# Score matmuls of two differential heads in one run of 24, and one pool of six PSUM banks for products and scores

## The chip, the cores and the metric

One NeuronCore of a Trainium2 chip runs the whole program. The metric is the device time of one execution in microseconds; it is given as the median of several runs. The engines are named as the profile names them: PE is the matmul engine (PEld its weight loads), DVE the vector engine, ACT the scalar engine, POOL and SP the two that only set constants and issue transfers here.

## The reference, cut to what matters

Two layers of an encoder over 256 tokens of width 2048. Each layer has a differential attention of 8 heads, a latent attention (MLA) of 8 heads, a gate for each, an output product, a SwiGLU feed-forward and a gated per-layer embedding.

```python
h = rmsnorm(x, g_mix[i])
z = h @ w_in[i]
dq, dk, dv, cq, ckv, kr, ga, gb = jnp.split(z, split_at, axis=-1)
# differential attention: 8 heads, each with two halves (c) of width 64
scores = jnp.einsum('bqhcd,bkhcd->bhcqk', qb, kh).astype(jnp.float32) * scale
probs = jax.nn.softmax(scores, axis=-1)
weights = probs[:, :, 0] - lam * probs[:, :, 1]
return jnp.einsum('bhqk,bkhe->bqhe', weights.astype(v.dtype), v)
```

So each differential head needs two score maps (one for each half of 64 features), two softmaxes, and their weighted difference.

## The kernel before

Activations lie with features on the 128 partitions and the 256 tokens on the free axis, each as two fp32r parts side by side: a high part and the rest (`ua`, `ub`, `fa`, `fb` hold 2 x 256 columns). Weights come from HBM as pieces of 128 x 1024 (`piece`, lines 182 to 208): ACT makes the high part `whi` (line 201), DVE the rest `wlo` (line 78, the helper that records every DVE addition and subtraction). Both have a ring of three buffers, so the split of a piece waits until PE has finished the piece three before it. A product (`product`, line 234) multiplies 16 chunks of a weight tile with 16 chunks of activations into one PSUM bank: for each chunk a matmul of 512 columns with `whi` (line 226) and one of 256 columns with `wlo` (line 230). `joined` (line 254) then takes the product out of its bank: ACT copies one half (`join`, line 256), DVE adds the other half (`a`), and with that addition the bank is free. `pair` (line 246) makes two small products from one piece.

PSUM has eight banks. Before the change four of them are for products (pool `ps_mm`, tile `mm`), two for scores (`ps_s`, tile `S`) and two for transposes and outputs of heads (`ps_at`, tile `at`). A pool gives a tile one of its free banks when the program is built, and the first matmul into it waits for the last reader of what was there.

The differential stage comes once in each layer. `beside()` (line 617) is a list of fillers, cut into steps by its yields: two steps for each of the heads 2 to 7 (first `keys_up`, two small products for the latent keys, or `narrow` for the shared rope key, or nothing; then `queries_keys`, a query product and a key product with their rotation), and four steps with a gate and two small products each. `settle` (line 709) normalizes four heads' outputs. `pipelined` (line 718) weighs head h+1 between two steps and puts out head h after it. `diff_weights` (line 684) does one head: `scores` (line 420) runs its 12 score matmuls, `exps` (line 431) its two softmaxes (a DVE reduction for the row maxima, two ACT exponentials for each map), and then ACT scales and DVE combines the two maps. The score matmuls have 64 rows only; `scores` lets those of the two halves alternate, so that they lie on the upper and the lower half of the array and run side by side. `turned` (line 440) transposes the weights, and `diff_out` (line 695) multiplies them with the values.

The order within an engine is made by the build's scheduler from the order of the code, except where `tc.keep_in_program_order` fixes it. Each engine then works strictly in that order, with semaphores between the engines.

Of the kernel before, what the change touches and what calls it, by code (L numbers as in the profile page):

```python
# [15 lines left out]
AF = mybir.ActivationFunctionType  # L16
ALU = mybir.AluOpType
AX = mybir.AxisListType

P = 128  # L20
T = 256
# [3 lines left out]
DH = 8  # L25
# [31 lines left out]
def encoder(ctx, tc, x, p, positions, cols, lams, wq, wk, wv, wcq, wckv, wkr, wga, wgb,  # L57
            w_q_up, w_kn, w_v, w_bd, w_bm, w_out, w_gate, w_up, w_down, w_pin, w_pg, rope_c, out):
    nc = tc.nc
    V, A, PE = nc.vector, nc.scalar, nc.tensor  # L60
    PSUM = bass.MemoryType.PSUM
    pool = lambda name, bufs=1, **k: ctx.enter_context(tc.tile_pool(name=name, bufs=bufs, **k))
# [1 line left out]
    wts = pool("wts")  # L64
    tmp = pool("tmp")
    stat = pool("stat")
    ps_mm = pool("ps_mm", 4, space=PSUM)
    ps_s = pool("ps_s", 2, space=PSUM)
    ps_at = pool("ps_at", 2, space=PSUM)

    def scratch(tag, bufs, n=T):
# [2 lines left out]
    def bank(ps=ps_at, tag="at", name="at", shape=(P, 2 * T)):  # L74
        return ps.tile(list(shape), F32, tag=tag, name=name)
# [4 lines left out]
    def stt(o, a, s, b, op0, op1):  # L80
        return V.scalar_tensor_tensor(out=o, in0=a, scalar=s, in1=b, op0=op0, op1=op1)

    def ts(o, a, s1, s2, op0, op1=ALU.bypass):
        return V.tensor_scalar(out=o, in0=a, scalar1=s1, scalar2=s2, op0=op0, op1=op1)  # L84
# [16 lines left out]
    def operand(t):  # L101
        return t.rearrange("p c t -> p (c t)")
# [24 lines left out]
    halves = rc[:, 4 : 4 + P]  # L127
# [28 lines left out]
    neg_lam = const.tile([P, DEPTH], F32, name="neg_lam")  # L156
    gsub = const.tile([P, DEPTH], F32, name="gsub")
    lam_s = const.tile([P, DEPTH, 2], F32, name="lam_s")
    lam_in = tmp.tile([P, 2, T], F32, tag="E", name="lam_in", bufs=2).rearrange("p l (f d) -> p l f d", f=4)

# [212 lines left out]
    krs = [const.tile([P, gap + 2 * T], F32R, name=f"kr{j}")[:, gap:] for j, gap in enumerate((KR_GAP, 0))]  # L373
# [43 lines left out]
    def three(q, k):  # L417
        return [(q[:, :T], k[:, T:]), (q[:, T:], k[:, :T]), (q[:, :T], k[:, :T])]

    def scores(*maps):  # L420


        Ss = [bank(ps_s, "S", "S", (P, 2, T)) for _ in maps]
        for b in range(2):
            for j in range(len(maps[0])):
                for S, pairs in reversed(list(zip(Ss, maps))):
                    q, k = pairs[j]
                    PE.matmul(S[:, b, :], q[:, b * P : (b + 1) * P], k, start=j == 0, stop=j == len(pairs) - 1)  # L428
        return Ss

    def exps(S, E, scale):

        nm, sm, rs = (stat.tile([P, 2], F32, tag=t, name=t, bufs=4) for t in ("nm", "sm", "rsum"))
        V.tensor_reduce(out=nm, in_=S, axis=AX.X, op=ALU.max, negate=True)
        ts(nm, nm, scale, None, ALU.mult)
        for b in range(2):
            last_exp[0] = A.activation(E[:, b, :], S[:, b, :], AF.Exp, bias=nm[:, b : b + 1], scale=scale, accum_out=sm[:, b : b + 1])  # L437
        V.reciprocal(out=rs, in_=sm)
        return rs
# [17 lines left out]
    def head(vals, kb, h):  # L457
        return vals[:, kb, h // 4, (h % 4) * P : (h % 4 + 1) * P]

    def weights(tag="E", dt=F32):  # L460
        return tmp.tile([P, 2, T], dt, tag=tag, name=tag, bufs=2)
# [65 lines left out]
    for L in range(DEPTH):  # L527
# [43 lines left out]
        qk = [(ub[h], operand(fa(h, F32R))) for h in range(DH)]  # L571
# [13 lines left out]
        qn, kn, qr = [], [], ub[14:]  # L585
# [94 lines left out]
        fill = beside()  # L680
        od, ods = [], ub[:8]
        ssd = stat.tile([P, 2 * DH], F32, tag="ssd", name="ssd", bufs=1)

        def diff_weights(h):
            q, k = qk[h]
            E = [weights(), weights("E1")]
            halves = [slice(c * 64, (c + 1) * 64) for c in range(2)]
            r = [exps(S, e, 0.125) for S, e in zip(scores(*(three(q[d], k[d]) for d in halves)), E)]
            ts(r[1], r[1], neg_lam[:, L : L + 1], None, ALU.mult)
            for b in range(2):  # L690
                A.activation(E[0][:, b, :], E[0][:, b, :], AF.Copy, scale=r[0][:, b : b + 1])
                stt(E[0][:, b, :], E[1][:, b, :], r[1][:, b : b + 1], E[0][:, b, :], ALU.mult, ALU.add)
            return E[0]

        def diff_out(h, W):
            wt = turned(W)
            yield
            o = bank()
            for b in range(2):
                for kb in range(2):  # L700
                    PE.matmul(o[:, b * P : (b + 1) * P], wt[:, kb, b * P : (b + 1) * P], head(vd, kb, h), start=kb == 0, stop=kb == 1)  # L701
            f = fa(h)
            od.append(f[:, 0, :])
            A.activation(od[h], o[:, :T], AF.Copy)
            for b in range(2):
                A.activation(f[:, 1, :P], od[h][:, b * P : (b + 1) * P], AF.Square, accum_out=ssd[:, 2 * h + b : 2 * h + b + 1])
# [12 lines left out]
        def pipelined(weigh, put, heads, step):  # L719
            W = weigh(0)  # L720
            for h in range(heads):
                step()
                nxt = weigh(h + 1) if h + 1 < heads else None
                out = put(h, W)
                next(out)
                step()
                next(out, None)
                W = nxt

        pipelined(diff_weights, diff_out, DH, lambda: next(fill, None))  # L730
        for _ in fill:
            pass
        vm, = (v for v in values(w_v[L], ckv) if v is not None)
# [3 lines left out]
        def mla_weights(h):  # L737
            E = weights()
            t = slice(h % 2 * T, (h % 2 + 1) * T)
            S, = scores(three(qn[h], kn[h]) + [(qr[h // 2][:, t], krs[1][:, t]), (qr[h // 2][:, t], krs[0][:, :T])])  # L740
            r = exps(S, E, MLA_SCALE)
            for b in range(2):
                ts(E[:, b, :], E[:, b, :], r[:, b : b + 1], None, ALU.mult)
            return E
# [48 lines left out]
        for part, (f0, f1) in enumerate(FF_PARTS):  # L793
            for f in range(f0, f1):
# [50 lines left out]
    parts, banks, tiles_ = {}, {}, {}  # L845
# [14 lines left out]
    for n in ends:  # L860
        m = banks[n, 1] = bank(ps_mm, "mm", "mm")
# [40 lines left out]
    def transposed(b, q, into, c0=0, c1=4):  # L902
        for c in range(c0, c1):
            tc.keep_in_program_order(PE.transpose(into[:, c * P : (c + 1) * P], xT[:, 4 * q + c, b * P : (b + 1) * P], ident))  # L904
        return into
# [17 lines left out]
            scaled(o[:, k * 2 * T : (k + 1) * 2 * T], src, col, engine)  # L923
        tc.keep_in_program_order(nc.sync.dma_start(out[b, :, q * 2 * T : (q + len(srcs)) * 2 * T], o))

    def S_bank():
        return operand(bank(ps_s, "S", "S", (P, 2, T)))

    def mm_bank():
        return bank(ps_mm, "mm", "mm")  # L930

    def steps(which, n):
        for _ in range(n):
            tc.keep_in_program_order(next(which))
# [6 lines left out]
    column = factors(0)  # L941
    for which, n in ((column, 2), (third, 1), (column, 2), (second, 1), (column, 1), (second, 1), (column, 1), (third, 1), (column, 1), (third, 1), (column, 1)):
        steps(which, n)
    t0 = [transposed(0, q, get()) for q, get in enumerate((S_bank, S_bank, mm_bank, mm_bank))]
    t1 = [transposed(1, q, mm_bank()) for q in range(2)]
    steps(factors(1), 8)
    t1.append(transposed(1, 2, bank()))
# [1 line left out]
    with tc.issue_after(gains[-1].ins):  # L949
        for q, m in ((1, 1), (2, 2)):  # L950
            store(0, q, t0[q : q + m], cols_[0], (A, A))
    t1.append(transposed(1, 3, S_bank()))
    for q in (0, 2):
        store(1, q, t1[q : q + 2], cols_[1], (V, A))

# [87 lines left out]
```

## Time and profile before

| | |
|---|---|
| median of 3 runs | 2826.22 us (2826.18 to 2826.6) |
| the profiled execution, its own time | 2825.67 us |
| its span | 2823.8 us |
| PE busy | 2815.6 us (100% of the span) |
| DVE busy | 2078.3 us (74%) |
| ACT busy | 1532.2 us (54%) |
| runs of 12 score matmuls of 64 rows | 16 (8 in a layer), 192 matmuls |
| differential stage, layer 0 / layer 1 | first score run at 106.12 us / at 1509.42 us |

PE is busy from 1 us to the end, so the time is the sum of what PE's instructions take from one to the next. What is not PE matters only where it makes PE wait. A view of groups gives the mean duration of an instruction. Instructions of DVE and ACT overlap a little with the next, so the distance from one start to the next, which the timeline shows, is shorter than that duration.

### The profile page before, as it was taken

The numbers are of one execution on the slowest core, as the hardware profiler recorded it, in microseconds if no ns is written. First come the engines' busy times: TensorE is split into PE (matmuls) and PEld (weight loads), VectorE is DVE, ScalarE is ACT, GpSimd is POOL, SyncE is SP. The second block draws the span as 40 slices with busy tenths as digits, with TensorE's granted clock in tenths as the row PEclk, the third lists the DMA queues.
The fourth block names the chain that finished last, engine by engine and source line by source line (L and its number), as shares of the span: only waits on it lengthen the run. The fifth ranks groups of instructions, "written<-read, shape, count | busy, mean of one in ns | idle before, by whom it ended". The sixth has DMA issues, their size and how long they took to land.

```text
span 2823.8 us, 43997 instructions
## 1 busy us (share of the span) xinstructions
PE 2815.6 (100%) x16691; PEld 2488.8 (88%) x16691; DVE 2078.3 (74%) x3574; ACT 1532.2 (54%) x2556; POOL 2.0 (0%) x16
## 2 busy tenths in 40 slices
PE   9999999999999999999999999999999999999998
PEld 8888988888888888888888889888888888888888
DVE  8898668776666666677869976687766666666777
ACT  7676556554444444455646765465544444444556
POOL 0000000000000000000000000000000000000000
PEclk9999999999999999999999999999999999999999
DMA  7544455555665565565664454555556655655654
GB/s 247 176 160 172 158 186 197 194 194 194 187 200 194 187 195 199 193 192 193 194 194 165 157 173 159 194 197 193 193 194 189 200 193 185 202 195 193 192 193 154
DMA packets 158325, 531.37 MB, mean 188 GB/s; under 512 B 17184, under 2 KB 25376, under 8 KB 158112
## 3 DMA queue, kind: packets, MB, share of 16 engines
q1 hardware_dynamic: 157680, 527.96, 56.9%
q8 instruction: 131, 2.15, 0.3%
q14 instruction: 82, 0.67, 0.1%
q10 hardware_dynamic: 432, 0.59, 0.1%
HBM read 526.39 MB, written 2.10 MB: 187 GB/s over the span
## 4 chain that ended last, share of the span: by engine, by line
PE 100%; DVE 0%; DVEq 0%; issue 0%
PE mm L226 61%; PE mm L230 31%; PE S L428 1%; PE mmv L502 1%; PE mmv L503 1%; PE mmv L501 1%; PE at L446 1%; PE at L701 1%; PE mm L848 0%; PE at L757 0%; PE mm L414 0%; PE at L517 0%; PE at L716 0%; PE mmv L472 0%; PE at L339 0%; PE mm L904 0%
## 5 line engine op out<-in xcount | busy, mean ns | idle before, releaser
L201 ACT ACTIVATE whi<-w 128x1024 fp32r<-128x1024 f32 (+2 forms) x1038 | 1064.2, 1026 | 1226.7 <-issue 593.3
L78 DVE TENSOR_TENSOR wlo<-w,whi 128x1024 fp32r<-128x1024 f32 (+2 forms) x1038 | 1224.7, 1180 | 647.9 <-ACT whi L201 640.5
L226 PE MATMUL mm<-ub,whi 128*128 128x512 f32 x3936 | 1340.5, 389 | 0.0
L226 PE MATMUL mm<-ua,whi 128*128 128x512 f32 x3712 | 1274.0, 390 | 0.0
L230 PE MATMUL mm<-ub,wlo 128*128 128x256 f32 x3936 | 1084.6, 276 | 0.0
L230 PE MATMUL mm<-ua,wlo 128*128 128x256 f32 x3712 | 1027.6, 277 | 0.0
L226 PEld LDWEIGHTS mm<-ub,whi 128*128 128x128 f32 x3936 | 737.8, 188 | 152.7
L226 PEld LDWEIGHTS mm<-ua,whi 128*128 128x128 f32 x3712 | 696.3, 188 | 141.5
L230 PEld LDWEIGHTS mm<-ub,wlo 128*128 128x128 f32 x3936 | 738.9, 188 | 1.3
L230 PEld LDWEIGHTS mm<-ua,wlo 128*128 128x128 f32 x3712 | 697.0, 188 | 2.0
L78 DVE TENSOR_TENSOR a<-mm,join 128x256 f32<-128x256 f32 (+1 forms) x423 | 174.2, 415 | 1.7 <-ACT join L877 1.4
L256 ACT ACTIVATE join<-mm 128x256 f32<-128x256 f32 x452 | 165.2, 367 | 6.4 <-PE mm L230 5.7
L78 DVE TENSOR_TENSOR xT<-xT,mm 128x256 f32<-128x256 f32 x256 | 106.7, 419 | 41.5 <-PE mm L230 37.7
L78 DVE TENSOR_TENSOR a<-a,row 128x256 f32<-128x256 f32 (+1 forms) x209 | 87.4, 422 | 5.9
L78 DVE TENSOR_TENSOR a<-a 128x256 f32<-128x256 f32 x120 | 50.8, 425 | 4.0
L78 DVE TENSOR_TENSOR ua<-a,ua 128x256 fp32r<-128x256 f32 x120 | 49.8, 417 | 1.0 <-ACT ua L264 1.0
L264 ACT ACTIVATE ua<-a 128x256 fp32r<-128x256 f32 x120 | 48.2, 403 | 2.6 <-DVE a L78 2.6
L437 ACT ACTIVATE E<-S,nm 128x256 f32<-128x256 f32 x96 | 44.1, 471 | 8.2 <-DVE nm L84 8.2
L501 PE MATMUL mmv<-whi,ua 128*128 128x512 f32 x124 | 47.0, 391 | 0.0
L502 PE MATMUL mmv<-whi,ua 128*128 128x512 f32 x124 | 47.0, 392 | 0.0
L503 PE MATMUL mmv<-wlo,ua 128*128 128x512 f32 x124 | 41.2, 391 | 0.0
L78 DVE TENSOR_TENSOR ssq<-ssq,sq 128x256 f32<-128x256 f32 x96 | 40.0, 417 | 0.3 <-ACT sq L294 0.3
(213 smaller groups left out, 1211.8 us busy)
## 6 DMA issues: line engine op xcount, KB each, us to landing
w<-in_w_gate SPq DMA_DIRECT2D x176, 512.0 KB, 4.6
w<-in_w_up SPq DMA_DIRECT2D x176, 512.0 KB, 4.6
w<-in_w_down SPq DMA_DIRECT2D x128, 512.0 KB, 4.3
w<-in_wga SPq DMA_DIRECT2D x64, 512.0 KB, 3.8
w<-in_wgb SPq DMA_DIRECT2D x64, 512.0 KB, 3.7
w<-in_w_out SPq DMA_DIRECT2D x64, 512.0 KB, 4.5
w<-in_w_pg SPq DMA_DIRECT2D x64, 512.0 KB, 4.7
w<-in_w_down SPq DMA_DIRECT2D x64, 384.0 KB, 3.6
```

The costliest lines, as they stand in the source:

```text
L78: return V.tensor_tensor(out=o, in0=a, in1=b, op=op)
L201: last_split[:] = A.activation(hi[:, s], w[:, s], AF.Copy), tt(lo[:, s], w[:, s], hi[:, s].bitcast(F32), ALU.subtract)
L226: lead = PE.matmul(acc, hi[:, s], u, start=start, stop=False)
L230: rest = PE.matmul(acc[:, T:], lo[:, s], u[:, :T], start=False, stop=stop)
L256: A.activation(t, acc[:, T:], AF.Copy)
L264: return A.activation(hi, src, AF.Copy), tt(lo, src, hi.bitcast(F32), ALU.subtract)
L428: PE.matmul(S[:, b, :], q[:, b * P : (b + 1) * P], k, start=j == 0, stop=j == len(pairs) - 1)
L437: last_exp[0] = A.activation(E[:, b, :], S[:, b, :], AF.Exp, bias=nm[:, b : b + 1], scale=scale, accum_out=sm[:, b : b + 1])
L446: PE.transpose(tp[:, kb, b * P : (b + 1) * P], W[:, b, kb * P : (kb + 1) * P], ident)
L501: PE.matmul(banks[k][b], xh, hi[:, s], start=c == 0, stop=False)
L502: PE.matmul(banks[k][b], xl, hi[:, s], start=False, stop=False)
L503: last_mm[:] = [PE.matmul(banks[k][b], xh, lo[:, s], start=False, stop=c == n - 1)]
```

## The change

1. `ps_s` is gone, and `ps_mm` has six banks in place of four. A score map takes a bank of the same pool as a product.
2. `scores` takes several heads and runs them one after the other, kept in program order where there is more than one. `diff_weights(h0)` takes the heads h0+1 and h0: 24 score matmuls in four banks, and then both heads' softmaxes.
3. A written loop over pairs of heads replaces `pipelined` in the differential stage: two steps at first; then for each pair the scores, two steps (one for the last pair), the transposes of both heads, one step, both heads' outputs, and one step (none for the last pair). So a pair's scores stand one or two steps after the keys of its second head.
4. The transposes at the end of the kernel take banks of the pool of six where they took score banks.

The MLA stage calls `scores` with one head and one map, as before.

```diff
-    ps_mm = pool("ps_mm", 4, space=PSUM)
-    ps_s = pool("ps_s", 2, space=PSUM)
+    ps_mm = pool("ps_mm", 6, space=PSUM)
...
-    def scores(*maps):
-        Ss = [bank(ps_s, "S", "S", (P, 2, T)) for _ in maps]
-        for b in range(2):
-            for j in range(len(maps[0])):
-                for S, pairs in reversed(list(zip(Ss, maps))):
-                    q, k = pairs[j]
-                    PE.matmul(S[:, b, :], q[:, b * P : (b + 1) * P], k, start=j == 0, stop=j == len(pairs) - 1)
+    def scores(*heads):
+        Ss = [[S_bank() for _ in maps] for maps in heads]
+        for banks, maps in zip(Ss, heads):
+            for b in range(2):
+                for j in range(len(maps[0])):
+                    for S, pairs in reversed(list(zip(banks, maps))):
+                        q, k = pairs[j]
+                        m = PE.matmul(S[:, b, :], q[:, b * P : (b + 1) * P], k, start=j == 0, stop=j == len(pairs) - 1)
+                        if len(heads) > 1:
+                            tc.keep_in_program_order(m)
         return Ss
...
-        def diff_weights(h):
-            q, k = qk[h]
-            E = [weights(), weights("E1")]
+        def diff_weights(h0):
             halves = [slice(c * 64, (c + 1) * 64) for c in range(2)]
-            r = [exps(S, e, 0.125) for S, e in zip(scores(*(three(q[d], k[d]) for d in halves)), E)]
+            pairs = [[three(qk[h][0][d], qk[h][1][d]) for d in halves] for h in (h0 + 1, h0)]
+            Ws = []
+            for Ss in scores(*pairs):
+                E = [weights(), weights("E1")]
+                r = [exps(S, e, 0.125) for S, e in zip(Ss, E)]
...
+                Ws.append(E[0])
+            return Ws[::-1]
...
-        pipelined(diff_weights, diff_out, DH, lambda: next(fill, None))
+        steps_on(2)
+        for h in range(0, DH, 2):
+            last = h + 2 == DH
+            Ws = diff_weights(h)
+            steps_on(1 if last else 2)
+            outs = [diff_out(h + j, Ws[j]) for j in range(2)]
+            for part in outs:
+                next(part)
+            steps_on(1)
+            for part in outs:
+                next(part, None)
+            if not last:
+                steps_on(1)
```

How the instructions stand after the change, at three places of layer 0 (layer 1 has the same). Lines of the changed kernel are shifted: its 77 is line 78 of before, 225 and 229 are 226 and 230, 437 is 428, 445 is 434, 588 is 577, 730 is 716.

**PE, around the first score run.** Before, the run of head 0 stands within the small products for the latent keys (`ub` 104 and 105 are the latent, `ua` the normalized input):

```order
L226 MATMUL mm<-ub_104,whi 128x512
L230 MATMUL mm<-ub_104,wlo 128x256
L428 MATMUL S<-fa_640,ub_92 128x256 x12
L226 MATMUL mm<-ub_105,whi 128x512
L230 MATMUL mm<-ub_105,wlo 128x256
L226 MATMUL mm<-ub_104,whi 128x512
```

Now the run of 24 (first head 1, then head 0) stands behind the key product of head 2. Behind it come the two small products `mm_1473` and `mm_1485` of the next step, 8 matmuls, and then the query product of head 3, `mm_1497`:

```order
L225 MATMUL mm_1473<-ub12_101,whi_1469 128x512 [waits PE_49]
L229 MATMUL mm_1473<-ub12_101,wlo_1468 128x256
L225 MATMUL mm_1473<-ub13_102,whi_1469 128x512
L229 MATMUL mm_1473<-ub13_102,wlo_1468 128x256
L225 MATMUL mm_1485<-ub12_101,whi_1469 128x512 [waits DVE_49]
L229 MATMUL mm_1485<-ub12_101,wlo_1468 128x256
L225 MATMUL mm_1485<-ub13_102,whi_1469 128x512
L229 MATMUL mm_1485<-ub13_102,wlo_1468 128x256
L225 MATMUL mm_1497<-ua0_73,whi_1500 128x512 [waits DVE_49]
```

The run has moved 72 matmuls later and is twice as long. Its four score maps hold four of the six banks, `mm_1473` and `mm_1485` get the other two, and `mm_1497` is given the bank of `mm_1473`. The wait on DVE in the last row is for the addition that takes `mm_1473` out of that bank.

**DVE, at the same place.** Before, the two reductions of head 0 stand between additions, and the addition that frees the bank of the small product (`mm_1297`) comes a few rows behind them, long before that bank is wanted again:

```order
L434 TENSOR_REDUCE nm_1270<-S_1256 128x2
L434 TENSOR_REDUCE nm_1278<-S_1257 128x2
L78 TENSOR_TENSOR ub9_101<-fb5_648,ub9_101 128x256
L78 TENSOR_TENSOR ub10_102<-fb6_649,ub10_102 128x256
L78 TENSOR_TENSOR ub11_103<-fb6_649,ub11_103 128x256
L78 TENSOR_TENSOR ub1_93<-a_1171,ub1_93 128x256
L577 STREAM_SHUFFLE sh_1246<-a_1244 128x256
L78 TENSOR_TENSOR a_1305<-mm_1297,join_1303 128x256
```

Now the addition out of `mm_1473` is the last of these rows. `wlo_1521` is the second half of head 3's query weights, `mm_1337` the key product of head 2 that PE ends just before the run, `mm_1393` to `mm_1396` are the score maps:

```order
L77 TENSOR_TENSOR wlo_1521<-w32_1520,whi_1522 128x1024
L77 TENSOR_TENSOR a_1384<-mm_1337,join_1382 128x256
L77 TENSOR_TENSOR a_1328<-a_1328,sh_1330 128x256
L445 TENSOR_REDUCE nm_1423<-mm_1393 128x2
L445 TENSOR_REDUCE nm_1431<-mm_1394 128x2
L588 STREAM_SHUFFLE sh_1386<-a_1384 128x256
L445 TENSOR_REDUCE nm_1446<-mm_1395 128x2
L77 TENSOR_TENSOR ub2_91<-a_1328,ub2_91 128x256
L445 TENSOR_REDUCE nm_1454<-mm_1396 128x2
L83 TENSOR_SCALAR nm_1423<-nm_1423 128x2
L83 TENSOR_SCALAR nm_1431<-nm_1431 128x2
L77 TENSOR_TENSOR a_1481<-mm_1473,join_1479 128x256
```

Four reductions, a weight split and six smaller instructions now stand ahead of the addition that frees the bank. At the second pair (heads 2 and 3) DVE has the same picture: `mm_1729` is the key product ahead of the run, and PE's query product `mm_1889`, behind the two small products `mm_1865` and `mm_1877`, waits for the last row:

```order
L77 TENSOR_TENSOR wlo_1913<-w32_1912,whi_1914 128x1024
L77 TENSOR_TENSOR a_1776<-mm_1729,join_1774 128x256
L445 TENSOR_REDUCE nm_1815<-mm_1785 128x2
L445 TENSOR_REDUCE nm_1823<-mm_1786 128x2
L445 TENSOR_REDUCE nm_1838<-mm_1787 128x2
L588 STREAM_SHUFFLE sh_1778<-a_1776 128x256
L445 TENSOR_REDUCE nm_1846<-mm_1788 128x2
L83 TENSOR_SCALAR nm_1815<-nm_1815 128x2
L77 TENSOR_TENSOR a_1873<-mm_1865,join_1871 128x256
```

Behind the third run stands the product of `narrow` (16 matmuls of 512 columns), which takes one bank, and the next product's bank is freed by an addition that stands ahead of the four reductions.

**PE, at the last pair.** The run of heads 6 and 7 is cut in two by a pair of transposes of 128 rows that belong to `settle`:

```order
L229 MATMUL mm<-ub_100,wlo 128x256
L437 MATMUL mm<-fa_644,ub_96 128x256 x7
L730 MATMUL at<-ident,fa_2029 128x128 x2
L437 MATMUL mm<-fa_644,ub_96 128x256 x5
L437 MATMUL mm<-fa_643,ub_95 128x256 x12
L225 MATMUL mm<-ua_73,whi 128x512
```

So a layer has five stretches of 64-row matmuls where it had eight, and the cut falls between the two matmuls of a side-by-side pair.

More of the change, by code (lines that the diff above doesn't have):

```diff
@@ L418, in three, with mm_bank, S_bank @@
         return [(q[:, :T], k[:, T:]), (q[:, T:], k[:, :T]), (q[:, :T], k[:, :T])]
-    def scores(*maps):
-        Ss = [bank(ps_s, "S", "S", (P, 2, T)) for _ in maps]
-        for b in range(2):
-            for j in range(len(maps[0])):
-                for S, pairs in reversed(list(zip(Ss, maps))):
-                    q, k = pairs[j]
-                    PE.matmul(S[:, b, :], q[:, b * P : (b + 1) * P], k, start=j == 0, stop=j == len(pairs) - 1)
+    def mm_bank():
+        return bank(ps_mm, "mm", "mm")
+    def S_bank():
+        return mm_bank().rearrange("p (b t) -> p b t", b=2)
+    def three(q, k):
+        return [(q[:, :T], k[:, T:]), (q[:, T:], k[:, :T]), (q[:, :T], k[:, :T])]
+    def scores(*heads):
[8 more added lines that the diff above has]
+                            tc.keep_in_program_order(m)
         return Ss
@@ L682, in encoder @@
         ssd = stat.tile([P, 2 * DH], F32, tag="ssd", name="ssd", bufs=1)
-        def diff_weights(h):
-            q, k = qk[h]
-            E = [weights(), weights("E1")]
+        def diff_weights(h0):
             halves = [slice(c * 64, (c + 1) * 64) for c in range(2)]
-            r = [exps(S, e, 0.125) for S, e in zip(scores(*(three(q[d], k[d]) for d in halves)), E)]
[L689 to L693, printed above, removed]
+            pairs = [[three(qk[h][0][d], qk[h][1][d]) for d in halves] for h in (h0 + 1, h0)]
[3 more added lines that the diff above has]
+                r = [exps(S, e, 0.125) for S, e in zip(Ss, E)]
+                ts(r[1], r[1], neg_lam[:, L : L + 1], None, ALU.mult)
+                for b in range(2):
+                    A.activation(E[0][:, b, :], E[0][:, b, :], AF.Copy, scale=r[0][:, b : b + 1])
+                    stt(E[0][:, b, :], E[1][:, b, :], r[1][:, b : b + 1], E[0][:, b, :], ALU.mult, ALU.add)
+                Ws.append(E[0])
+            return Ws[::-1]
         def diff_out(h, W):
@@ L728, in pipelined, with steps_on @@
                 W = nxt
-        pipelined(diff_weights, diff_out, DH, lambda: next(fill, None))
+        def steps_on(n):
+            for _ in range(n):
+                next(fill)
+        steps_on(2)
[11 more added lines that the diff above has]
+                steps_on(1)
         for _ in fill:
@@ L739, in mla_weights @@
             t = slice(h % 2 * T, (h % 2 + 1) * T)
-            S, = scores(three(qn[h], kn[h]) + [(qr[h // 2][:, t], krs[1][:, t]), (qr[h // 2][:, t], krs[0][:, :T])])
+            (S,), = scores([three(qn[h], kn[h]) + [(qr[h // 2][:, t], krs[1][:, t]), (qr[h // 2][:, t], krs[0][:, :T])]])
             r = exps(S, E, MLA_SCALE)
@@ L924, in store @@
         tc.keep_in_program_order(nc.sync.dma_start(out[b, :, q * 2 * T : (q + len(srcs)) * 2 * T], o))
[L926 to L930, printed above, removed]
     def steps(which, n):
@@ L943, in encoder @@
         steps(which, n)
-    t0 = [transposed(0, q, get()) for q, get in enumerate((S_bank, S_bank, mm_bank, mm_bank))]
+    t0 = [transposed(0, q, get()) for q, get in enumerate((mm_bank,) * 4)]
     t1 = [transposed(1, q, mm_bank()) for q in range(2)]
@@ L951, in encoder @@
             store(0, q, t0[q : q + m], cols_[0], (A, A))
-    t1.append(transposed(1, 3, S_bank()))
+    t1.append(transposed(1, 3, mm_bank()))
     for q in (0, 2):
```

## Prediction

> **What bounds the kernel now.** I read the page first, then PE's waits, then the chain that ended last, and at last the timeline of the differential stage.
>
> ```profile
> PE 2815.6 (100%) x16691; PEld 2488.8 (88%) x16691; DVE 2078.3 (74%) x3574; ACT 1532.2 (54%) x2556; POOL 2.0 (0%) x16
> PEclk9999999999999999999999999999999999999999
> ```
>
> ```profile
> engine line waited for: us in total, times, longest us
> PE at L517 <- DVE ones L123: 1.0, 1, 1.0
> ```
>
> PE is never idle but for 1.0 us at the start, its granted clock is full throughout, and the second view, PE's own waits, has that one row. So the change can gain only by making PE's instructions follow each other more closely, and it loses whatever wait it gives PE, microsecond for microsecond. Where can instructions follow more closely? The chain, in pieces in order of time (start, us), shows what a run of score matmuls costs beyond its work:
>
> ```profile
> 106.19 0.91 PE S L428 x12
> 107.10 0.43 PE mm L226
> 107.53 0.12 PE mm L230
> 107.65 0.23 PE mm L226
> ```
>
> ```profile
> 138.07 0.90 PE S L428 x12
> 138.98 0.59 PE at L446 x4
> ```
>
> ```profile
> 322.25 1.18 PE S L428 x10
> 323.43 0.44 PE at L446 x4
> ```
>
> The third piece is an MLA run: ten full-height matmuls of 256 columns in 1.18 us, 0.118 each. Two half-height ones side by side take as long as one of these, so twelve should take 6 x 0.117 = 0.70 us. They take 0.91, which is 0.21 more, and what follows is late as well: a product matmul takes 0.43 in place of 0.23 (0.20 more), four transposes 0.59 in place of 0.44 (0.15 more). **A run of half-height matmuls therefore costs 0.41 us of entering and leaving before a product and 0.35 before transposes**, however long it is.
>
> DVE has no part in the chain, but it is full just where the change works:
>
> ```profile
> core 0: us, PE busy (x) PEld busy (x) DVE busy (x) ACT busy (x) POOL busy (x), PEclk, DMA share, GB/s
> 95.00:105.00 10.00, 10.00 (x63) 8.91 (x62) 9.86 (x25) 5.00 (x11) 0.00 (x0) 1.00 0.60 196
> 105.00:115.00 10.00, 10.00 (x67) 8.65 (x66) 10.00 (x24) 8.30 (x18) 0.00 (x0) 1.00 0.29 101
> 115.00:125.00 10.00, 10.00 (x68) 8.64 (x67) 10.00 (x27) 8.30 (x19) 0.00 (x0) 1.00 0.62 209
> 125.00:135.00 10.00, 10.00 (x64) 8.97 (x63) 9.60 (x26) 7.68 (x23) 0.00 (x0) 1.00 0.55 173
> ```
>
> From 105 to 125 us DVE works 20.0 of 20 us. It doesn't stop PE, because what PE needs from it is always done a little earlier. A wait of PE for something that stands far back in DVE's row would not be hidden.
>
> **Part 1: fewer runs.** Before, a layer has eight runs, five followed by transposes and three by products: 5 x 0.35 + 3 x 0.41 = 2.98 us. After, it has three whole runs and one that is cut by two transposes, five stretches in all, four followed by products: 4 x 0.41 + 0.35 = 1.99. The cut leaves two half-height matmuls without a partner, which adds one matmul's time, 0.12: 2.11. Each layer gains 0.87 us, both **1.7 us**. What crossing from one head to the next inside a run costs isn't in the trace; heads alternate halves there as within a head, so it lies between nothing and the 0.21 of a new run, and I take nothing.
>
> **Part 2: the wait for a bank.** Four score maps fill four of the six banks. The next step is two small products of four matmuls each, in the other two. The query product behind them gets the bank of the first small product, so PE waits until DVE has added that product out. Count from the moment at which PE ends the key product ahead of the run.
>
> PE, from rows above: entering and leaving 0.41, twelve pairs 12 x 0.117 = 1.40, and four times a product's pair of 0.23 + 0.11 for the small products, 1.36. PE is at the query product after **3.16 us**.
>
> For DVE take the distances between starts, from the timeline:
>
> ```profile
> 106.87 1.23 DVE L78 TENSOR_TENSOR wlo<-w,whi 128x1024 fp32r<-128x1024 f32 x1
> 108.01 0.41 DVE L78 TENSOR_TENSOR a<-mm,join 128x256 f32<-128x256 f32 x1
> 108.35 0.41 DVE L78 TENSOR_TENSOR ub<-fb,ub 128x256 fp32r<-128x256 f32 x1
> 108.68 1.28 DVE L434 TENSOR_REDUCE nm<-S 128x2 f32<-128x512 f32 x2
> 109.88 1.08 DVE L78 TENSOR_TENSOR ub<-fb,ub 128x256 fp32r<-128x256 f32 x3
> ...
> 111.23 0.44 DVE L577 STREAM_SHUFFLE sh<-a 128x256 f32<-128x256 f32 x1
> 111.57 0.40 DVE L78 TENSOR_TENSOR a<-mm,join 128x256 f32<-128x256 f32 x1
> 111.89 0.15 DVE L84 TENSOR_SCALAR nm<-nm 128x2 f32<-128x2 f32 x1
> 111.95 1.22 DVE L78 TENSOR_TENSOR wlo<-w,whi 128x1024 fp32r<-128x1024 f32 x1
> ```
>
> A weight split takes 1.14 us (106.87 to 108.01), an addition or a shuffle 0.34, two reductions 1.20 (108.68 to 109.88), a tiny scaling 0.07. The first row of DVE's list, `wlo_1521`, cannot start earlier than the count: its piece takes the ring buffer of the key product's second half, three pieces back, and ACT's `whi` must go first. That ACT waits for PE in this way is ordinary here:
>
> ```profile
> ACT whi L201 <- PE mm L226: 16.1, 14, 2.3
> ```
>
> ```profile
> L201 ACT ACTIVATE whi<-w 128x1024 fp32r<-128x1024 f32 x36 | 38.3, 1064 | 19.9 <-PE mm L226 16.1 <-issue 1.2 <-ACT join L256 0.9
> ```
>
> These are rows of 95 to 225 us (the first of the waits from 105 on); 14 of ACT's splits there began when PE released a buffer, and one takes 1.06 us. So the addition out of `mm_1473` is done after
>
> - 1.06 (`whi_1522`) + 1.14 (`wlo_1521`) = 2.20
> - + 0.34 + 0.34 (`a_1384`, `a_1328`) = 2.88
> - + 4 x 0.60 (reductions) + 0.34 (shuffle) + 0.34 (`ub2`) + 2 x 0.07 = 6.10
> - + 0.41, the whole of `a_1481` = **6.51 us**.
>
> PE waits 6.51 - 3.16 = 3.35 us. At the second pair two additions and one scaling fewer stand ahead: 2.20 + 0.34 + 2.40 + 0.34 + 0.07 + 0.41 = 5.76, and PE waits 2.60 us. At the third pair `narrow` stands behind the run, and there and at the fourth the next whole product takes a bank that was emptied ahead of the reductions, so I cost both at nothing. Closest is the second half of the fourth run, whose banks come from the gate product 2.7 us (8 x 0.34) ahead of it: one split and one addition later, 2.20 + 0.41 = 2.6 us, that bank is free. A layer loses 5.95 us, both **11.9 us**.
>
> Two bounds on this. Is DVE free when `whi_1522` is done? In the new order 21 rows stand from 108.68 on ahead of that split, 17 of 0.34, three weight splits of 1.14 and one of half the width, about 0.6: 108.7 + 9.8 = 118.5. The key product ends at 105.7 + 36 x 0.34 = 117.9, so the split can start at 119.0, and DVE is free by 0.5. If it is not, each wait grows by what it is late, at most about 0.5. And what PE needs to start again behind a semaphore isn't shown in this trace; it is between nothing and a weight load that isn't hidden:
>
> ```profile
> L226 PEld LDWEIGHTS mm<-ub,whi 128*128 128x128 f32 x3936 | 737.8, 188 | 152.7
> ```
>
> That is 0.19 us, four times 0.75. Loads run ahead of matmuls nearly everywhere here, so I take nothing.
>
> **Part 3: what hides.** The softmaxes of two heads must end before the transposes. PE has 64 product matmuls (10.9 us) behind the wait, and DVE behind that addition some 6.5 us of rows to the last weighted difference, by the same distances; ACT's eight exponentials lie beside these. If that cover of 4 us were gone, PE would wait there too. The keys of the second head are split one step earlier than the scores want them, except at the first pair, where DVE is done with them about when PE arrives; a wait there only moves the larger one. Two more banks for products elsewhere gain nothing, since PE waits for no bank now. The end of the kernel gets the same number of free banks as before.
>
> **The sum.** 2825.67 - 1.7 + 11.9 = 2835.9 us for the profiled execution. The median of the runs is 0.55 us above it: **2836.4 us**, slower by 0.36%. A measurement of this kernel can tell about 0.2%, 5.7 us, from no change.
>
> **The rivals.**
>
> *It does what it says.* The runs merge and no wait comes: 2826.2 - 1.7 = 2824.5 us, no difference that can be measured. This needs the addition to be done 3.16 us after the key product. The four reductions alone can't start before the run's first half ends, 1.0 us in, and take 2.4; with the additions ahead and behind there are no 3.16 us unless the scheduler's order isn't the one that runs. 7%.
>
> *The split doesn't stand in the way.* If `whi` and `wlo` of the second half find a free buffer earlier, DVE begins with the addition at once, and each wait is shorter by up to 2.20: (1.15 + 0.40) x 2 = 3.1 us lost, 1.7 gained, 2827.6 us. Against it stands that ring and rows are in a fixed order, and 16.1 us of ACT's waits for PE. 5%.
>
> *PE's clock falls in the waits.* Four waits of 2.6 to 3.4 us are the first of any length since the start, and at the start PE is slow:
>
> ```profile
> 1.05 3.78 PE at L517 x16
> ```
>
> That is 0.24 us a matmul of 128 columns, where the transposes of the same width above take 0.44 / 4 = 0.11. If a wait brought such a stretch back, some 1.9 us would be lost behind each: 2836.4 + 4 x 1.9 = 2844 us, or 2840.2 if only the two longer ones do it. The profile of before has no wait to show it. 8%.
> [...]
>
> **How the numbers follow.** The forecast has 80%: 2831 to 2841 holds it, with the waits 1 us shorter or longer each, the 0.5 us of a late DVE and the 0.19 us of a load. Of the clock's 8% about half lies below 2841. The range leaves out the two cheap cases (12%) and the rest of the clock's. Faster by over 0.2% (below 2820.6) needs a gain that no row shows: 2%. Within 0.2% (up to 2831.9) are the cheap cases and the forecast's low end: 13%. Slower: 85%.
>
> **What would show it.** PE's waits in the new profile should have four rows or so for DVE's addition, two of about 3.3 us and two of about 2.6, at the query products of heads 3 and 5 in both layers, 12 us together. The granted clock should stay full. Runs of 24 should take 1.6 us, and PE's matmuls between them should be as far apart as before. If PE has no new wait, part 2 is wrong; if the waits sit at the transposes or at the scores, part 3 is; if there are waits at the third or fourth pair, I mis-costed these.

## The result, and the profile after

| | before | after |
|---|---|---|
| median of 6 runs each | 2826.20 us (2825.84 to 2826.65) | 2840.39 us (2839.75 to 2841.91) |
| the profiled execution, its own time | 2825.67 us | 2841.91 us |
| its span | 2823.8 us | 2840.1 us |
| PE busy | 2815.6 us | 2820.9 us |

The ratio of the times is 1.005, with a 95% interval of 1.004 to 1.006: the kernel is slower by 14.2 us. The forecast was 2836.4, slower by 10.2.

First the page and PE's waits after the change (what waited, on what, us in total, times, longest).

```profile
PE 2820.9 (99%) x16691; PEld 2494.7 (88%) x16691; DVE 2080.2 (73%) x3574; ACT 1534.2 (54%) x2556; POOL 2.0 (0%) x16
```

```profile
engine line waited for: us in total, times, longest us
PE mm L225 <- DVE a L77: 9.8, 4, 2.9
PE mm L437 <- DVE fa L77: 1.1, 2, 0.7
PE at L528 <- DVE ones L122: 1.1, 1, 1.1
```

Where there was one short wait (1.0 us at the start, still there in the last row), there are now four of a query product for DVE's addition, and two small ones of the first run of scores for the keys. With as many matmuls as before, PE is also *busy* for 5.3 us longer. Waits don't explain that, and it is the part that the forecast lacked.

The timeline of PE shows the first of the four in place (start, us, what, and the idle time before it).

```profile
118.84 0.28 PE L229 MATMUL mm<-ua,wlo 128*128 128x256 f32 x1
119.51 1.69 PE L437 MATMUL mm<-fa,ub 64*128 64x256 f32 x24 [0.39 <-DVE fa L77]
121.13 0.50 PE L225 MATMUL mm<-ub,whi 128*128 128x512 f32 x1
...
122.51 0.28 PE L229 MATMUL mm<-ub,wlo 128*128 128x256 f32 x1
125.66 0.50 PE L225 MATMUL mm<-ua,whi 128*128 128x512 f32 x1 [2.87 <-DVE a L77]
```

The run of 24 takes 1.62 us from its start to the next product (119.51 to 121.13). The small products follow, and then PE is idle until 125.66. The chain that ended last shows what it waited for, and what it met behind the wait.

```profile
119.09 1.07 ACT whi L200
120.18 1.23 DVE wlo L77
121.41 0.67 DVE a L77 x2
122.07 1.13 DVE nm L445 x2
123.21 0.42 DVE sh L588
123.63 0.57 DVE nm L445
124.46 0.68 DVE nm L445
125.28 0.34 DVE a L77
125.66 0.50 PE mm L225
...
127.20 0.43 PE mm L225
...
130.28 0.23 PE mm L225
```

Read down: the split, two additions, the reductions, and last the addition that frees the bank, as forecast. Behind the wait a product matmul takes 0.43 us in place of 0.23, until about 130 us. The view by windows says why. I lay it on a raster of 3.41 us, which is the length of each of the three stretches of low clock that this trace has between its start and its end (columns: PE, PEld, DVE, ACT, POOL busy, the granted clock, share and rate of DMA).

```profile
119.75:123.16 3.41, 3.04 (x32) 2.46 (x30) 3.26 (x6) 1.72 (x5) 0.00 (x0) 1.00 0.50 145
123.16:126.58 3.42, 0.92 (x5) 0.83 (x6) 3.42 (x13) 3.39 (x8) 0.00 (x0) 1.00 0.33 114
126.58:129.99 3.41, 3.41 (x12) 2.83 (x11) 2.97 (x11) 3.41 (x15) 0.00 (x0) 0.50 0.36 123
129.99:133.40 3.41, 3.41 (x21) 3.02 (x20) 2.88 (x8) 3.02 (x8) 0.00 (x0) 1.00 0.08 31
...
157.30:160.71 3.41, 1.32 (x7) 1.19 (x8) 3.41 (x12) 2.89 (x9) 0.00 (x0) 1.00 0.40 137
160.71:164.12 3.41, 3.41 (x12) 2.83 (x12) 3.13 (x12) 3.41 (x16) 0.00 (x0) 0.50 0.44 147
1532.87:1536.28 3.41, 2.04 (x16) 1.45 (x13) 3.41 (x9) 2.07 (x5) 0.00 (x0) 1.00 0.50 169
1536.28:1539.69 3.41, 2.14 (x12) 1.90 (x13) 3.41 (x12) 3.40 (x11) 0.00 (x0) 1.00 0.01 2
1567.00:1570.41 3.41, 1.28 (x7) 0.91 (x6) 3.41 (x12) 2.67 (x8) 0.00 (x0) 1.00 0.42 145
1570.41:1573.83 3.42, 3.42 (x12) 2.86 (x12) 3.13 (x12) 3.42 (x14) 0.00 (x0) 0.50 0.38 126
```

Three times a window with PE busy for 0.92 to 1.32 us is followed by one at a clock of 0.50: PE is busy for all of its 3.41 us, but with 12 matmuls in place of 21. Half of 3.41 us, about 1.7 us, is lost each time. The remaining wait (1534.7 to 1537.55, the first of layer 1) lies across the border of two windows, 2.04 and 2.14 us busy, and no fall follows.

Put together from the starts of the same matmuls in both profiled executions (a wait is the distance between two starts less the usual one):

| us | layer 0 | layer 1 |
|---|---|---|
| first run waits for the keys | 0.46 | 0.74 |
| first pair's query product waits for the bank | 3.03 | 2.80 |
| second pair's | 2.33 | 2.29 |
| falls of the clock | 2 x 1.7 = 3.4 | 1.7 |
| fewer runs, what is left over | -0.6 | -0.8 |
| measured, start to end of the stage | 8.6 | 6.7 |

With 1.0 us at the very start, where this execution reached the full clock 2.2 us later than that of before (7.1 and 4.9 us in), this makes 16.3 us; the two own times differ by 16.24. The row of what is left over is a remainder: it holds the gain of the fewer runs, if there is one, and whatever the price of 1.7 us for a fall is off by. PE has no wait at the third and fourth pair, and outside the two stages and the start the same matmuls are as far apart as before.

### The profile page after: what moved, and what is told of

Same layout as the page of the kernel before. It is cut to its first block, busy times and chain, and to the rows that moved or that the text cites. A ratio compares the mean times of both kernels' runs of the same rounds, so it can differ in the third digit from the quotient of the medians.

```text
span 2840.1 us, 43907 instructions
## 1 busy us (share of the span) xinstructions
PE 2820.9 (99%) x16691; PEld 2494.7 (88%) x16691; DVE 2080.2 (73%) x3574; ACT 1534.2 (54%) x2556; POOL 2.0 (0%) x16
## 3 DMA queue, kind: packets, MB, share of 16 engines
q8 instruction: 130, 2.13, 0.3%
## 4 chain that ended last, share of the span: by engine, by line
PE 99%; DVE 1%; issue 0%; ACT 0%; DVEq 0%
PE mm L225 61%; PE mm L229 31%; PE mmv L513 1%; PE mmv L514 1%; PE mmv L512 1%; PE mm L437 1%; PE at L715 1%; PE at L457 0%; PE mm L878 0%; PE at L787 0%; DVE nm L445 0%; PE mm L413 0%; DVE wlo L77 0%; ACT whi L200 0%; PE mmv L483 0%
## 5 line engine op out<-in xcount | busy, mean ns | idle before, releaser
L448 ACT ACTIVATE E<-mm,nm 128x256 f32<-128x256 f32 x96 | 44.6, 477 | 12.3 <-DVE nm L83 12.3
```

## The experiments

Times are medians; the kernel before ran beside each of them and took 2826.0 to 2826.2 us.

**Fill the bank waits (e1, e10).** Two kernels give PE work that needs nothing where it would wait for the bank, for 2.1 us.

```diff
+        def busy(n):
+            b_ = bank()
+            for _ in range(n):
+                tc.keep_in_program_order(PE.matmul(b_[:, :P], ones_r, ones_r, start=True, stop=True))
...
-            steps_on(1 if last else 2)
+            steps_on(1)
+            if h < 4:
+                busy(18)
+            if not last:
+                steps_on(1)
```

> As the changed kernel, but behind the small products of the first two pairs of heads PE gets 18 matmuls of 128 columns on the tile of ones, which need nothing: by the half of the 0.24 us that one takes at the start under a clock of 0.5, 0.12 each, 2.1 us of each bank wait are filled. The bank itself comes no earlier. Theory (the waits bring the clock down to 0.5 for 3.4 us, which costs 1.7 us each time): waits of about 0.9, 0.2, 0.7 and 0.2 us are left, PE is at the query product at the same moment as before, the clock stays full, and the time falls by what three drops cost, about 5 us, to 2835 to 2836. Rival (the clock falls for another reason, the length of the runs or their place): the drops stay, and the time stays at 2840 or grows.

Measured: 2837.04 us (2836.16 to 2838.25), ratio 1.0039 [1.0026, 1.0051]. PE's waits and three windows of its profiled execution, 2838.25 us:

```profile
PE mm L225 <- DVE a L77: 2.0, 4, 0.9
PE mm L437 <- DVE fa L77: 1.1, 2, 0.7
```

```profile
118.91:122.33 3.42, 3.16 (x34) 2.89 (x34) 3.27 (x8) 1.73 (x4) 0.00 (x0) 1.00 0.52 170
122.33:125.74 3.41, 2.46 (x21) 2.27 (x21) 3.41 (x12) 3.38 (x7) 0.00 (x0) 1.00 0.46 144
125.74:129.15 3.41, 3.41 (x13) 2.93 (x12) 3.22 (x12) 3.41 (x15) 0.00 (x0) 0.50 0.25 76
```

The waits are what was expected, and extra work that computes nothing makes the kernel 3.4 us faster than the change: two of the three falls of the clock are gone together with most of PE's idleness (the granted clock of the profiled execution is 0.999 in the mean, 0.998 in that of the change). In this execution, the slowest of the five, one fall of three is left, at the first pair, a window at 0.50 behind one in which PE is busy for 2.46 us, 2.05 of them with the fillers. Whether the other executions had it, and with it why the median is 1 us above the forecast, isn't shown.

In the second kernel the fillers are about as long (2.25 us in place of 2.12 by PE's timeline), but nine wide ones:

```diff
-                tc.keep_in_program_order(PE.matmul(b_[:, :P], ones_r, ones_r, start=True, stop=True))
+                tc.keep_in_program_order(PE.matmul(b_, ones_r, ua[0], start=True, stop=True))
```

> As the run that filled the bank waits with 18 matmuls of 128 columns, but with 9 of 512 columns on an operand of the products, 0.23 us each by the products' rows, the same 2.1 us. In that run one fall of the clock was left, behind a stretch of 3.41 us in which PE was busy for 2.46 us by the profile, 1.9 of them with the small fillers. Theory (what keeps the clock up is the work of the array, and a matmul of 128 columns with its weight load has little of it): no fall, waits of 0.9, 0.2, 0.7 and 0.2 us as there, and 2826.2 - 1.5 + 11.7 = 2836.4 us or up to 1 us less, with less spread than there. Rival (any wait of about 1 us can bring the clock down, by its place alone): a fall is left at the first pair, 2837 to 2838.

Measured: 2837.38 us (2837.10 to 2838.85). The granted clock of the profiled execution is 0.999 in the mean, and the 512-column matmuls on `ua` take 395 ns on average from 118 to 160 us, where e1 with its fall has 411. Two bank waits are left, 1.3 us in all, at the first pairs. A stage without a fall agrees with the theory, but the time is 1 us above what it forecast, in the rival's range, and no better than with the small fillers. So the two kernels' times don't decide between theory and rival; of one profile each, e1's shows a fall at the first pair and e10's none there. The bank waits differ as well, four of 2.0 us in all in e1, so what brings the clock down isn't shown by this pair.

**Reductions behind the addition (e2).** The softmaxes are written behind the step of small products, and the row maxima of the first two pairs are made to issue behind the addition out of the first small product.

```diff
+        with ExitStack() as stack:
+            if behind:
+                stack.enter_context(tc.issue_after(behind[0].ins))
+            V.tensor_reduce(out=nm, in_=S, axis=AX.X, op=ALU.max, negate=True)
-        V.tensor_reduce(out=nm, in_=S, axis=AX.X, op=ALU.max, negate=True)
...
-            Ws = diff_weights(h)
-            steps_on(1 if last else 2)
+            maps = diff_scores(h)
+            if not last:
+                steps_on(1)
+            behind[:] = adds[-2:-1] if h < 4 else []
+            Ws = diff_weights(maps)
+            behind.clear()
+            steps_on(1)
```

> As the changed kernel, but in the first two pairs of heads DVE's four row maxima stand behind the addition out of the first small product (three rotations of 0.34 us move ahead of it in their place at the first pair, two at the second). Theory (the bank is freed by an addition that stands behind the reductions): the bank waits of 3.0 and 2.3 us shrink to about 1.5 and 0.5, the clock stays full, the two waits ahead of the first run (0.5 and 0.7 us) stay: 2826.2 - 1.7 + 4.0 + 1.2 = 2829.7 us. Rival (the weight split alone decides, the reductions would fit beside it): waits stay at 2.3 us or more and the time at 2838 or more. If waits of 1.5 us still bring the clock down, 2833.

Measured: 2834.27 us (2833.84 to 2835.63), ratio 1.0030 [1.0018, 1.0041].

```profile
PE mm L225 <- DVE a L77: 4.3, 4, 1.5
PE mm L229 <- DVE wlo L77: 1.8, 2, 0.9
PE mm L437 <- DVE fa L77: 0.8, 2, 0.4
```

The bank waits shrink from 9.8 to 4.3 us, near the forecast of 4.0, and the granted clock is 0.999 in each of the six runs (0.997 or 0.998 in those of the change): the reductions ahead of the addition were the larger part of the wait. But there are two new waits of 0.9 us for DVE's splits, which the later reductions probably push back, and the median lies 4.6 us above the forecast. 1.8 of that are these waits; the rest, in a stage in which transposes and outputs now stand in smaller pieces between products, is not traced here.

**One ring of eight banks (e3).**

```diff
-    ps_mm = pool("ps_mm", 6, space=PSUM)
-    ps_at = pool("ps_at", 2, space=PSUM)
+    ps_mm = pool("ps_mm", 8, space=PSUM)
```

> As the changed kernel, but the transposes and outputs share one ring with products and scores: all eight banks, handed out in turn. The query product behind the small products now gets the bank of the query product ahead of the run, which was added out before the run. Theory (the whole loss comes from the bank wait and the clock behind it): no bank wait and a full clock, the waits ahead of the first run stay: 2826.2 - 1.7 + 1.2 = 2825.7 us, less 0.3 to 0.5 a layer if the last run isn't cut, 2825 in all. Rival (runs of 24 or the order around them cost by themselves): 2830 or more without any wait of PE for an addition. Other rival: in one ring transposes or products wait for a bank that a late output holds; then PE shows new waits for ACT.

Measured: 2877.77 us (2877.13 to 2879.02), ratio 1.0183 [1.0170, 1.0197]. The largest of PE's waits:

```profile
PE at L729 <- DVE fa L82: 14.6, 2, 7.3
PE at L456 <- DVE E L79: 8.3, 5, 3.7
PE at L378 <- DVE a L76: 7.8, 2, 3.9
PE at L714 <- ACT wt L461: 3.3, 3, 1.5
```

The query products behind the first two runs wait no more for an addition, as expected. The time is a miss, 52 us above the forecast. The scheduler, free to hand out more banks, now places transposes earlier, and PE stands at them until their data is there: those of line 378, for instance, stand in layer 0 16 matmuls behind the third run, where the change has 49. The granted clock is lower, too, 0.993 in the profiled execution. As a test of the bank it agrees; as a kernel it suggests that the two rings also held the order together.

**The run one step earlier (e4).**

```diff
-        steps_on(2)
+        steps_on(1)
...
-            steps_on(1 if last else 2)
+            steps_on(2)
```

> As the changed kernel, six banks too, but each run of 24 stands one step earlier, behind the small products and ahead of the whole query and key products, so that the two free banks go to these, and the bank of the next small product is wanted some 22 us later. Theory (the bank wait needs the small products behind the run): no bank wait, a full clock, 2826.2 - 1.7 = 2824.5 us, up to 1 us more or less by where the last run is cut. Rival (four score banks out of six are too many wherever the run stands): waits of 2 us or more for DVE's additions remain, 2835 or more. Other rival: the softmaxes have the same cover, but the scores want the second head's keys one step sooner, and PE waits ahead of the runs for DVE's split, 1 to 3 us each.

Measured: 2866.70 us (2866.57 to 2867.91), ratio 1.0144 [1.0128, 1.0159].

```profile
PE mm L437 <- DVE fa L77: 31.0, 6, 7.7
```

The bank wait is gone, and the last rival holds with a larger price than I gave it: the runs of the first three pairs wait for the second head's keys, 3.7 to 7.7 us each, and the granted clock is 0.993 in each of the four executions. The second step of distance in the change is what the keys need.

**Six banks, heads one by one (e5).**

```diff
-        steps_on(2)
-        for h in range(0, DH, 2):
...
+        pipelined(diff_weights, diff_out, DH, lambda: next(fill, None))
```

> One part of the change alone: six banks for products and scores in one ring, but the differential heads weighed one by one in runs of 12, each one step of work behind its keys, as before the change. Two banks go to scores at a time, so the next products always find one that was emptied long ago. Theory (the loss belongs to four score banks taken at once ahead of the small products): no wait of PE for an addition, a full clock, 2826 us, 1 us more or less by the order that the scheduler now finds. Rival (scores in the ring of the products cost by themselves, since a product waits for a softmax's bank): waits of PE for ACT's exponentials or DVE's additions, 2830 us or more.

Measured: 2911.28 us (2909.88 to 2912.30), ratio 1.0301 [1.0286, 1.0315]. A miss:

```profile
PE mm L437 <- DVE fa L77: 21.5, 8, 4.4
PE at L457 <- DVE E L80: 18.1, 2, 9.1
PE at L712 <- ACT wt L462: 12.9, 9, 1.8
```

No wait is for a product's bank, so the theory's time isn't met, and the rival's is met without its mechanism. Single heads are not pinned to the order of the code, and with six banks to choose from the scheduler gives another order: ahead of the runs that wait, at most eight matmuls of small products, and transposes and outputs, stand behind the key product. The kernel says nothing of what the pool costs by itself, only that the pool decides the order too.

**Whole products first (e6).** At heads 3 and 5 the step behind the run makes the query and key product, and the small products after it.

```diff
+                if h in (3, 5):
+                    queries_keys(h)
+                    yield
                 if h < 6:
                     keys_up(2 * h - 4)
                 elif h == 7:
                     rotated(joined(narrow(wkr[L], ua)), crm, srm)
                 yield
+                if h in (3, 5):
+                    continue
                 queries_keys(h)
                 yield
```

> As the changed kernel, runs of 24 at the same place, but at heads 3 and 5 the step behind the run makes the whole query and key products first and the small products after them. The two free banks then go to the whole products, 22 us of work, and the first small product takes the first score bank, whose exponentials are read long before. DVE has the same rows. Theory (what is paid is the wait for the bank of the small product, and the clock behind it): no bank wait, a full clock; the waits for the second head's keys ahead of the first run (0.43 and 0.71 us) stay: 2826.0 - 1.7 + 1.1 = 2825.4 us. Since DVE's order changes around it and the transposes stand behind more small pieces, 1 us a layer may come on top: up to 2827.5. Rival (DVE is full there, and whatever stands behind the run waits for it): waits of 2 us or more at another place behind the first two runs, and 2832 or more.

Measured: 2832.70 us (2831.66 to 2833.16), ratio 1.0022 [1.0013, 1.0031].

```profile
PE mm L225 <- ACT whi L200: 3.6, 2, 3.3
PE mm L229 <- DVE wlo L77: 0.8, 1, 0.8
```

No bank wait in either layer, and in layer 0 the stage takes 0.2 us more than before the change. Layer 1 takes 5.5 more: new waits of 3.3 us for ACT's split and 0.8 for DVE's behind it, with the granted clock at 0.84 from 1535 to 1540 us. By its numbers, a wait of 2 us or more and a time of 2832 or more, the rival is met, though the engine waited for first is ACT and not DVE. ACT's timeline there shows it behind the exponentials of both heads:

```profile
1529.49 1.28 ACT L448 ACT_TABLE_LOAD   x1 [1.24 <-DVE nm L83]
1530.78 0.47 ACT L448 ACTIVATE E<-mm,nm 128x256 f32<-128x256 f32 x1
...
1533.94 0.51 ACT L448 ACTIVATE E<-mm,nm 128x256 f32<-128x256 f32 x1
...
1535.50 1.09 ACT L200 ACTIVATE whi<-w 128x1024 fp32r<-128x1024 f32 x1
```

In layer 0 that split stands ahead of the exponentials. The next run but one tests whether this is all.

**The last run uncut (e7).** As e6, and the eight transposes of `settle`, of which four cut the last run in e6, are pinned behind it.

```diff
-                if n == 0:
+                if n == 2:
                     settle(0)
...
-                    PE.transpose(t[:, b * P : (b + 1) * P], o, ident)
+                    m = PE.transpose(t[:, b * P : (b + 1) * P], o, ident)
+                    if h0 == 0:
+                        tc.keep_in_program_order(m)
```

> As the run with the whole products first, and the eight transposes that settle the first four heads stand behind the last run, pinned there, so that they don't cut it. Expected by the price of a stretch: 0.35 us for one of two stretches ahead of transposes and 0.12 for two matmuls that find their partner, 0.47 a layer, 0.9 us less than the run beside it, 2824.5 us. If entering and leaving a run of half-height matmuls costs nothing by itself, the time is that of the run beside it.

Measured: 2833.41 us (2832.74 to 2833.84), not faster than e6. The last run is whole (1.61 us), but layer 0, with the same waits in both, is 0.14 us longer than in e6 by the starts of its matmuls. The 0.47 us did not come. The transposes now stand behind the run and between products in three pieces, at a price that I had not counted; that entering and leaving a run costs nothing that a kernel can save, the other outcome that was named, isn't excluded.

**The small products aside (e8).** The order of the change, but these small products take the two banks of the other ring.

```diff
-            acc = bank(ps_mm, "mm", "mm")
+            acc = bank() if aside else bank(ps_mm, "mm", "mm")
...
-            for acc in pair(w_kn[L, n : n + 2], ckv):
+            for acc in pair(w_kn[L, n : n + 2], ckv, n in (2, 6)):
```

> As the changed kernel, but the small products of heads 3 and 5 go into the two banks of the ring for transposes and outputs, which nothing uses there; the whole products behind them get the two free banks of the six. At the first pair the small products then stand ahead of the run, at the second behind it as in the changed kernel; elsewhere the order is nearly the same. Theory (which bank the query product gets is the whole cause, and the clock falls only behind waits): no wait of PE for an addition, a full clock, 2826.2 - 1.7 = 2824.5 us, up to 1.1 more if the waits for the second head's keys ahead of the first run stay. Rival (DVE, full there, holds PE up anyway): waits of 2 us or more behind the first two runs, 2832 or more. Other rival (the merging gains nothing): no wait, and 2826.2.

Measured: 2827.62 us (2827.30 to 2828.14), ratio 1.0004 [0.9995, 1.0013]; 12.8 us faster than the change.

```profile
PE mm L229 <- DVE wlo L77: 1.5, 2, 0.8
PE at L528 <- DVE ones L122: 1.1, 1, 1.1
```

No wait for an addition is left, the granted clock is 0.999 in each of the eleven runs, and nearly all of the loss is gone, though the time is 2 to 3 us above the theory's 2824.5 to 2825.6; 1.5 us of that are the waits in the first row. The second pair is the clean test: PE's and DVE's orders around the run are those of the change, the addition out of the small product still stands behind the four reductions, and only the bank of the query product differs. PE's and DVE's timelines there:

```profile
152.03 0.28 PE L229 MATMUL at<-ub,wlo 128*128 128x256 f32 x1
152.14 0.39 PE L225 MATMUL mm<-ua,whi 128*128 128x512 f32 x1
```

```profile
154.36 0.41 DVE L77 TENSOR_TENSOR a<-at,join 128x256 f32<-128x256 f32 x1
```

The addition that the query product waited for in the change ends at 154.77, and PE has begun that product at 152.14, right behind the small ones. The wait of 2.3 us is gone in both layers. At the first pair the scheduler also put the small products ahead of the run and their addition ahead of the reductions, so there two things changed at once; two waits of 0.8 us for a split are left behind that run.

**Exponentials behind the split (e9).** As e6, and at the first pair the softmaxes issue behind the last split of the key product.

```diff
...
+            if h == 0:
+                steps_on(1)
+                with tc.issue_after(last_split[0].ins):
+                    Ws = diff_weights(maps)
...
```

> As the run with the whole products first, but at the first pair ACT's eight exponentials stand behind the last weight split of the key product in both layers; there, they stood so in the first layer only, and in the second PE waited 3.4 and 1.0 us for that split, with one fall of the clock. Theory (that is the whole of what the run with the whole products first lost): the second layer costs what the first did, 0.2 us: 2826.2 + 0.4 = 2826.6. Rival (the second layer loses it for another reason, late weights): 2832 to 2833 again.

Measured: 2826.88 us (2826.25 to 2827.26), ratio 1.0002 [0.9993, 1.0011]. Both layers now cost 0.2 us each, as the theory said, and the granted clock is 0.999 or 1.0 in each of the eleven runs. So the wait of e6 was ACT's order, and the rival of late weights falls.

## Why the prediction was right, and what it left out

**Part 1, fewer runs: the runs are right, the gain is not shown.** Runs of 24 take 1.61 us (1.6 said), the pieces of the cut ones 0.66 and 1.25. What is left over in the sum above is a gain of 1.4 us, 1.7 said, but as a remainder. No run shows it as time: in e9, where a wait of 0.3 us is all that the two stages have, each of them takes 0.2 us longer than before. Whether the gain is there and the order around the runs takes it back, or it never was, stays open.

**Part 2, the bank wait: right.** The chain forecast 6.51 us from the end of the key product to the end of the addition out of the first small product. In the profile `whi` starts at 119.09, and that addition stands in DVE's timeline as

```profile
125.20 0.41 DVE L77 TENSOR_TENSOR a<-mm,join 128x256 f32<-128x256 f32 x1
```

which makes 6.52 us. At the first pair PE loses 0.46 + 3.03 = 3.49 and 0.74 + 2.80 = 3.54 us (3.35 said), at the second 2.33 and 2.29 (2.60 said); 11.65 in all, 11.9 said. The third and fourth pair cost nothing, as said. That the bank is the cause is shown by the second pair of e8, and that the reductions are the larger part of what stands ahead of the addition by e2. The rival without the split falls: the chain goes through `whi` and `wlo`.

**Part 3: right.** PE waits at no transpose in the change. At the first run it waits for the keys, and that wait only moves part of the larger one, as the sums of 3.49 and 3.54 show.

**The step that failed is the sum.** It left the clock full, and gave "PE's clock falls in the waits" 8% as a rival. The falls that it named are there: three of about 1.7 us in the profiled execution (it had 1.9 for each). They follow neither all four waits nor the two longer ones: behind those of 3.03, 2.33 and 2.29 us there is one, behind that of 2.80, which lies across the border of two windows, none. That the measured 2840.39 is next to that rival's 2840.2 is chance. With the gain as forecast and the waits as measured, the sum for that execution is 2825.67 - 1.7 + 11.65 + 1.0 (the start) = 2836.6 us; three falls make it 2841.7, and it took 2841.91. For the median, filling the waits gave back 3.0 to 3.4 us, about two falls. That covers most of the 4.0 us by which the forecast was low. So the waits were foreseen for the right reason, but that the median still lies in the range, 0.6 us below its upper end, is partly luck: the range was not made for falls of the clock, and the profiled execution, the slowest of six, lies above it.

## What to carry to other kernels

When several banks of a ring are taken at once, ask which banks the next allocations get, and what stands ahead of their release on the engine that frees them; moving these allocations to another ring (e8) took back 12.8 of 14.2 us. Price a new wait of PE with the slow stretch that can follow it, here 1.7 us behind three of four waits of 2.3 to 3.0. And a pool that is widened or merged frees the scheduler to reorder: e3 and e5 lost 52 and 85 us against the kernel before, with waits for data, not for a product's bank, and a granted clock of 0.993 and 0.986 in their profiled executions (0.999 in that of before).

No version here beats the kernel before: e9 and e8 are level with it.

## What the hardware showed

In the profiled execution of the change the full clock begins 7.11 us after the start, and the three falls begin 35, 45 and 458 times 3.4133 us later (119.47, 153.60 and 1563.31 us), each 3.413 us long: all on one raster. Of its windows at the four bank waits three had 2.49, 2.09 and 2.13 us of PE's idle time in sum (3.41 less the busy time in the rows above), and each was followed by a window at 0.50. The two at the wait of 2.80 us had 1.37 and 1.27 us idle, and no fall followed. In e1, the run with the small fillers, a window with 0.95 us idle was followed by one at 0.50. So PE's idle time in a window, as the profile counts it, doesn't alone decide in these runs.

The full clock was reached 4.9 us after the start in the profiled execution of before and 7.1 in that of after, which made 1.0 us there. Whether the six runs of the change differ by that isn't shown: they spread over 2.2 us and those of the kernel before over 0.8, but the 18 runs of before beside e5 to e7 over 1.9.
